# A two-layer conv and attention diffusion block: adaLN sums on four column parts of TensorE, and a rearranged start

## Chip, cores and metric

One core of one Trainium2 chip. The metric is device time in microseconds (us) of one execution; the kernel before takes 1625.7 us (median of 3 runs, 1624.08 to 1625.84).

## What is computed

The reference runs two layers over 512 latent tokens `x` and 256 context tokens `ctx`, width 1024. Layer 0 mixes tokens by a gated convolution of three taps, layer 1 by neighbourhood attention with 16 heads; each is followed by a SwiGLU with 2816 hidden columns. Every sub-layer is modulated by adaLN: a shift, a scale and a gate come from `silu(cond)` through one matrix per layer. Cut to that part:

```python
for i in range(DEPTH):
    mod   = jax.nn.silu(c)     @ w_ada[i] + b_ada[i]      # latent tokens:  1024 -> 6 * 1024
    mod_c = jax.nn.silu(c_ctx) @ w_ada[i] + b_ada[i]      # context tokens
    sh1, sc1, g1, sh2, sc2, g2 = jnp.split(mod, 6, axis=-1)   # and so for mod_c
    h = rms_norm(x, norm_mix[i]) * (1 + sc1) + sh1        # ctx the same way
    x = x + g1 * mixer(h)                                 # convolution (i = 0), attention (i = 1)
    x = x + g2 * swiglu(rms_norm(x, norm_ffn[i]) * (1 + sc2) + sh2)
```

## The kernel before

The streams lie transposed, features on partitions: `x` is eight tiles of 128 x 512, `c` eight of 128 x 256. Every large product is made of three matmuls: weights and activations are split into a high and a low part (`split`, L134 on ScalarE and L135 on VectorE; tiles `wh`/`wl` or `ah`/`al` for weights, `hxh`/`hxl` for the normed x), and `mm3` (L188) adds high*high, high*low and low*high in PSUM. A scheduler orders what is not pinned by `in_order`; loads go out on SP's queue, and their buffers (`raw`, three of 1 MB) set when.

**Start of layer 0.** SP loads x (8 x 256 KB), then the first adaLN weights (`first_load`, L224: `raw`, four rows of 256 columns to a partition and DMA, so rows of 1 KB), then the first conv weights (`first_weights`, L617: `fraw`, 12 x 256 KB, rows of 1 KB). The squares of x are taken on VectorE and ScalarE and added up on VectorE (L371 to L382), and `stats` (L394) sums them over partitions on TensorE, in four column parts j: output partitions 32j to 32j+31. `first_sum` (L236) computes 512 of the adaLN columns for both conditions with 32-column weights `cs` = silu(cond), in two parts (`part` 0 and 1) of 16 matmuls of 128 columns, for each column part j all k in a row:

```python
for j in range(4):
    for k in range(part * nk, part * nk + nk):
        matmul(ps[32*j:32*j+32, :wd], cs[:, k, :], raw[:, kk, ...])     # L236
```

`first_finish` copies the sum to SBUF (L243), transposes it (L246) and makes shift and gain (L254, L256). `spread` (L409) broadcasts the norm, `apply` (L425, L427, L428) makes `hxh` and `hxl`. A loop over q = 0 to 3 does this for two x tiles at a time: `apply`, then the conv products of those two tiles (j = 0, 1, 2 for the three column groups c, u, b), with the `first_sum` of the next two tiles set between them.

**The other adaLN columns** (`Ada.step`, `_step`): 40 steps of one 1 MB load each; VectorE multiplies and adds into `aa` for the latent condition (L286, L288), ScalarE and GpSimd do the same for the context (L291, L294, L295). Every four steps `flush` sums over partitions on TensorE (L309): up to four accumulators (two column blocks j, one or two conditions c), with the weights `ones2`, which put condition c in column c, so that both conditions add into the same 32 partitions:

```python
for c in range(1 + both):
    for j, (_, _, _, accs) in enumerate(two):
        matmul(ps[32*j:32*j+32, :], ones2[:, c, :], accs[c], start=(c == 0), stop=(c == both))   # L309
```

`finish` copies 64 partitions (L315), transposes them in four pieces (L318) and adds the bias (L324). Six flushes have two conditions, the last four have one.

**Where steps stand.** In `swiglu` a step follows each of the hidden tiles (`tt`), and for the chunks but the last `residual` calls `along` after output tiles f = 0, 2, 4 (flush and step) and 6 (flush). The hidden tiles come in chunks of 6, 8 and 8 in layer 0; after each chunk `residual` multiplies by the output weights.

Of the kernel before, what the change touches and what calls it, by code (L numbers as in the profile page):

```python
# [15 lines left out]
P = 128  # L16
# [21 lines left out]
def dit_kernel(  # L38
# [6 lines left out]
    w_ada: bass.AP,  # L45
    conv_w_in: bass.AP,
    conv_w_out: bass.AP,
# [37 lines left out]
    ones2 = const.tile([P, 2, 32], F32, name="ones2")  # L85
    nc.vector.memset(ones2, 0.0)
    nc.vector.memset(ones2[:, 0, 0:1], 1.0)
    nc.vector.memset(ones2[:, 1, 1:2], 1.0)
# [8 lines left out]


    x_t = [xr.tile([P, NX], F32, name=f"x{f}") for f in range(KT)]
# [17 lines left out]

    def in_order(inst):
        return tc.keep_in_program_order(inst)
# [89 lines left out]
    class Ada:  # L209
# [7 lines left out]
        def first_load(self, k0, n, part):  # L217

            nk = 8 // n
            raw = wp.tile([P, 2048], F32, name="raw", tag="raw")  # L220
            raw = raw.rearrange("p (k w c) -> p k w c", k=nk, w=2)
            for w in range(2):
                c0 = w * D + k0 * P
                in_order(nc.sync.dma_start(  # L224
                    out=raw[:, :, w, :], in_=w_ada[0, part * nk * P:(part + 1) * nk * P, c0:c0 + n * P].rearrange(
                        "(k p) c -> p k c", p=P)))
            return raw

        def first_sum(self, n, part, raw):
# [70 lines left out]
        def flush(self):  # L300
# [6 lines left out]
            for c in range(1 + both):  # L307
                for j, (_, _, _, accs) in enumerate(two):
                    in_order(nc.tensor.matmul(self.ps[32 * j:32 * j + 32, :], ones2[:, c, :], accs[c],  # L309
                                              start=(c == 0), stop=(c == both)))  # L310
            self.finish(i, q // 2)

        def finish(self, i, g):
            row = nrm.tile([P, 512], F32, name="row", tag="row", bufs=1)
            nc.scalar.copy(out=row[0:64, :], in_=self.ps[0:64, :])  # L315
# [4 lines left out]
            tv = tp[:, 0:256].rearrange("p (s j m) -> p j s m", s=4, j=2)  # L320
            ba = vt[:, V_BADA + i * 48 + g * 8:V_BADA + i * 48 + g * 8 + 8].rearrange("p (j s) -> p j s", j=2)
            conds = range(2 if i == 0 or g < 2 else 1)
            for cond in conds:
                nc.vector.tensor_tensor(  # L324
                    out=mod[i][:, cond, g * 8:g * 8 + 8].rearrange("p (j s) -> p j s", j=2),
                    in0=tv[:, :, :, cond], in1=ba, op=ALU.add)
# [31 lines left out]
    class Norm:  # L358
# [27 lines left out]
        def stats(self, use="mm", ordered=True, urgent=False):  # L386
# [3 lines left out]
            with tc.high_priority() if urgent else nullcontext():  # L390
                st = bank(use, "st")
                for p, part in enumerate([self.a] + self.parts):
                    for j in range(4):
                        m = nc.tensor.matmul(st[32 * j:32 * j + 32, 0:ch], ones, part[:, j * ch:(j + 1) * ch],  # L394
                                             start=(p == 0), stop=(p == self.apart))
                        if ordered:
                            tc.keep_in_program_order(m)
                nc.vector.tensor_scalar(out=v, in0=st[:, 0:ch], scalar1=1.0 / D, scalar2=EPS,
                                        op0=ALU.mult, op1=ALU.add)
                nc.scalar.activation(out=self.y, in_=st[:, 0:ch], func=AF.Ln, scale=1.0 / D, bias=eps)  # L400
                e = nc.scalar.activation(out=self.y, in_=self.y, func=AF.Exp, scale=-0.5)
                self.ready = (e.ins, newton(v, self.y).ins)
# [64 lines left out]
    def swiglu(tmp, ap_, i, groups, hs, chunks, ada=None, begin=None, norms=None, out=None, end=None, begin_norm=None):  # L467
# [25 lines left out]
        for ci, n_t in enumerate(chunks):  # L493
# [43 lines left out]
            while tt < n_t:  # L537
# [9 lines left out]
                if ada is not None:  # L547
                    ada.step()
# [4 lines left out]
            along = {0: ada.also, 2: ada.also, 4: ada.also, 6: ada.flush} if ada is not None and not last else None  # L553
# [4 lines left out]
    with ExitStack() as l0:  # L558
# [47 lines left out]
        def first_weights(q, j):  # L606
            part = (1, 2, 0)[j]
# [8 lines left out]
            raw = raw[:, :512].rearrange("p (k c) -> p k c", k=2)  # L616
            in_order(nc.sync.dma_start(  # L617
# [16 lines left out]
        for f in range(KT):  # L634
            nX.square(f, nc.vector)
# [461 lines left out]
```

## Time and profile before

| | us |
|---|---|
| median of 3 runs | 1625.7 |
| the profiled execution, its own time | 1626.88 |
| its span in the trace | 1625.1 |
| TensorE matmul busy | 1592.8 |
| VectorE busy | 858.7 |
| ScalarE busy | 578.5 |
| GpSimd busy | 243.7 |
| mean load rate over the span | 99 GB/s |

The span is what lies between the first and the last instruction; the profiled execution is 1.78 us longer than it and 1.18 us over the median. PE is TensorE's matmuls, PEld its weight loads, DVE VectorE, ACT ScalarE, POOL GpSimd, SP the engine that issues most loads. Times in views run from the start of the span. A product in float32 stands in the trace as two matmul records.

### The profile page before, as it was taken

To read this page: it belongs to the slowest core of one execution; us is meant where nothing else is said; L and a number is where in the kernel's file an instruction comes from. 1 tells how busy PE (TensorE), PEld (TensorE's weight loads), DVE (VectorE), ACT (ScalarE), POOL (GpSimd) and SP (SyncE) were. 2 spreads that over 40 slices of the span, in tenths; PEclk is the share of its full clock that TensorE was granted. 3 is DMA by queue.
4 is the path that set the end of the run, shared out by engine and by line. 5 is a ranking of instruction groups with operands and counts; after the bars stand their busy time and mean duration, and the time that the engine had idled before them with its cause. 6 is when DMAs were issued, how large, how long until landed. Compare 5 with 4: busy or idle time off the path is not lost.

```text
span 1625.1 us, 22151 instructions
## 1 busy us (share of the span) xinstructions
PE 1592.8 (98%) x9132; PEld 1341.0 (83%) x9132; DVE 858.7 (53%) x1395; ACT 578.5 (36%) x967; POOL 243.7 (15%) x290
## 2 busy tenths in 40 slices
PE   6999999999999999999999999999999999999998
PEld 5898888888888888888888778788878888888887
DVE  5467667476654435343522766666787533333333
ACT  4243234354423221122222555555655332222231
POOL 0123226323422000000003211121111000000000
PEclk9999999999999999999999999999999999999999
DMA  9423343234434334233411121110121232223222
GB/s 315 139 78 130 104 144 116 78 104 149 136 104 130 125 109 156 76 127 105 147 65 53 47 71 59 33 59 28 60 87 55 78 104 92 90 88 119 78 84 72
DMA packets 137077, 162.35 MB, mean 100 GB/s; under 512 B 3216, under 2 KB 114064, under 8 KB 136976
## 3 DMA queue, kind: packets, MB, share of 16 engines
q1 hardware_dynamic: 133504, 156.66, 29.5%
q10 hardware_dynamic: 3472, 4.28, 0.8%
q8 instruction: 71, 1.16, 0.3%
q14 instruction: 30, 0.25, 0.1%
HBM read 158.84 MB, written 2.10 MB: 99 GB/s over the span
## 4 chain that ended last, share of the span: by engine, by line
PE 93%; DVE 3%; ACT 1%; DMA 1%; issue 1%; POOL 0%; SPq 0%; DVEq 0%; ACTq 0%
PE ps L188 83%; PE op L919 2%; PE tp L909 1%; PE ada_ps L236 1%; PE s L889 1%; DMA raw<-in_w_ada_dram 1%; PE ada_ps L309 1%; PE s L890 1%; PE stt L803 1%; DVE wl L135 1%; DVE t L425 0%; PE bc L409 0%; DVE hxl L428 0%; DVE aa L288 0%; DMA x<-in_xT_dram 0%
## 5 line engine op out<-in xcount | busy, mean ns | idle before, releaser
L188 PE MATMUL ps<-hxh,wh 128*128 128x512 f32 (+1 forms) x1128 | 435.8, 392 | 3.1 <-DVE q_sb L857 1.3
L188 PE MATMUL ps<-hxl,wh 128*128 128x512 f32 (+1 forms) x1128 | 432.3, 389 | 1.3 <-DVE hxl L428 1.3
L188 PE MATMUL ps<-hxh,wl 128*128 128x512 f32 (+1 forms) x1128 | 431.5, 388 | 0.7 <-DVE wl L135 0.7
L134 ACT CAST wh<-raw 128x1024 fp32r<-128x1024 f32 (+1 forms) x194 | 198.1, 1022 | 465.6 <-PE ps L188 418.6
L135 DVE TENSOR_TENSOR wl<-raw,wh 128x1024 fp32r<-128x1024 f32 (+1 forms) x194 | 241.8, 1247 | 184.1 <-ACT wh L134 180.8
L188 PEld LDWEIGHTS ps<-hxh,wh 128*128 128x128 f32 x1128 | 211.0, 189 | 54.0 <-issue 3.6
L188 PEld LDWEIGHTS ps<-hxh,wl 128*128 128x128 f32 x1128 | 212.1, 188 | 44.9 <-DVE wl L135 1.8
L188 PEld LDWEIGHTS ps<-hxl,wh 128*128 128x128 f32 x1128 | 211.8, 188 | 43.2 <-DVE hxl L428 2.5
L188 PE MATMUL ps<-ah,wh 128*128 128x512 f32 (+1 forms) x656 | 232.3, 354 | 2.5 <-ACT ah L134 2.5
L188 PE MATMUL ps<-al,wh 128*128 128x512 f32 (+1 forms) x656 | 231.9, 354 | 0.4 <-DVE al L135 0.4
L188 PE MATMUL ps<-ah,wl 128*128 128x512 f32 (+1 forms) x656 | 231.1, 353 | 0.0
L188 PE MATMUL ps<-hch,wl 128*128 128x256 f32 x648 | 181.4, 284 | 0.0
L188 PE MATMUL ps<-hcl,wh 128*128 128x256 f32 x648 | 180.6, 283 | 0.0
L188 PE MATMUL ps<-hch,wh 128*128 128x256 f32 x648 | 179.3, 283 | 0.0
L288 DVE SCALAR_TENSOR_TENSOR aa<-raw,cs,aa 128x512 f32<-128x512 f32 x140 | 144.1, 1030 | 41.1 <-DMA raw<-in_w_ada_dram 38.0
L295 POOL TENSOR_TENSOR aa<-aa,pr 128x512 f32<-128x512 f32 x84 | 135.6, 1615 | 183.6 <-ACT pr L294 109.6
L188 PEld LDWEIGHTS ps<-ah,wh 128*128 128x128 f32 x656 | 123.8, 189 | 24.9 <-issue 3.8
L188 PEld LDWEIGHTS ps<-al,wh 128*128 128x128 f32 x656 | 123.7, 189 | 18.4 <-DVE al L135 0.6
L188 PEld LDWEIGHTS ps<-ah,wl 128*128 128x128 f32 x656 | 123.8, 189 | 17.5
L441 DVE SCALAR_TENSOR_TENSOR x<-ps,mod,x 128x512 f32<-128x512 f32 (+1 forms) x80 | 55.1, 695 | 143.6 <-PE ps L188 143.6
L188 PEld LDWEIGHTS ps<-hch,wh 128*128 128x128 f32 x648 | 122.4, 191 | 3.3 <-issue 0.8
L188 PEld LDWEIGHTS ps<-hcl,wh 128*128 128x128 f32 x648 | 123.1, 192 | 2.0 <-issue 0.2
(170 smaller groups left out, 1577.1 us busy)
## 6 DMA issues: line engine op xcount, KB each, us to landing
raw<-in_ffn_w_in_dram SPq DMA_DIRECT2D x44, 1024.0 KB, 5.1
raw<-in_w_ada_dram SPq DMA_DIRECT2D x40, 1024.0 KB, 5.2
raw<-in_ffn_w_out_dram SPq DMA_DIRECT2D x16, 1024.0 KB, 4.9
raw<-in_attn_w_qkv_dram SPq DMA_DIRECT2D x12, 1024.0 KB, 5.3
raw<-in_conv_w_in_dram SPq DMA_DIRECT2D x9, 1024.0 KB, 5.3
raw<-in_w_ada_dram SPq DMA_DIRECT2D x16, 512.0 KB, 7.8
raw<-in_ffn_w_out_dram SPq DMA_DIRECT2D x8, 768.0 KB, 4.3
raw<-in_conv_w_out_dram SPq DMA_DIRECT2D x4, 1024.0 KB, 4.9
```

The source lines that it names most:

```text
L134: a = pinned(nc.scalar.copy(out=hi, in_=src))
L135: b = pinned(nc.vector.tensor_tensor(out=lo, in0=src, in1=hi.bitcast(F32), op=ALU.subtract))
L188: m = nc.tensor.matmul(ps, w[k][part], src[k], start=(first and k == i == 0), stop=(last and k == nk - 1 and i == 2))
L236: in_order(nc.tensor.matmul(self.ps[32 * j:32 * j + 32, :wd], self.cs[:, k, :], raw[:, kk, j // 2, j % 2 * wd:(j % 2 + 1) * wd], start=(k ...
L288: nc.vector.scalar_tensor_tensor(out=acc, in0=raw[:, kk, :], scalar=w, in1=acc, op0=ALU.mult, op1=ALU.add)
L295: nc.gpsimd.tensor_tensor(out=acc, in0=acc, in1=pr, op=ALU.add)
L309: in_order(nc.tensor.matmul(self.ps[32 * j:32 * j + 32, :], ones2[:, c, :], accs[c], start=(c == 0), stop=(c == both)))
L441: nc.vector.scalar_tensor_tensor(out=grp.tiles[f], in0=ps, scalar=modv(i, grp.cond, gate, f), in1=grp.tiles[f], op0=ALU.mult, op1=ALU.add)
L803: nc.tensor.matmul(stt[row:row + 32, :], ind, sq, start=True, stop=True)
L889: nc.tensor.matmul(s, qh[a][:, bs], keys(ks[a], w0), start=True, stop=False)
L890: nc.tensor.matmul(s, ql[a][:, bs], keys(ks[a], w0), start=False, stop=True)
L919: in_order(nc.tensor.matmul(op_[own, 0:P], vv[:, vi, own], tps[a][:, j * P:(j + 1) * P], start=(j == 0), stop=(j == 3)))
```

## The change

1. `first_sum` runs over k outside and the column parts j inside, so that four neighbouring matmuls write four different column parts.
2. `flush` gives each of its up to four accumulators a column part of its own, with the weights `ones`; `ones2` goes. `finish` copies and transposes 128 partitions where it was 64 (64 stay 64 for the one-condition flushes).
3. The host lays out the first adaLN weights (`w_ada1`, 8 x 128 x 2048) and the first conv weights (`conv_w1`, 12 x 128 x 512) as they lie on chip. One DMA of 1 MB with rows of 8 KB takes the place of two of 512 KB; the conv DMAs have rows of 2 KB.
4. x is loaded over SP's and ACT's queues in turn, and the first two adaLN loads go out on ACT's queue.
5. `stats_of_each`: all eight squares of x on VectorE, each summed by four matmuls as it comes.
6. In the loop over q `apply` has high priority and the splits of the conv weights are ordered behind given instructions (`after`).
7. In `swiglu` the step after the last hidden tile of a chunk goes (not in the last chunk), and `along` has a step after f = 1, flush and step after 3 and 5, and the flush after 6.

```diff
@@ x and the first adaLN loads
+    def first_load(q, part, queue=None):
+        raw = wp.tile([P, 2048], F32, name="raw", tag="raw")
+        in_order((queue or nc.sync).dma_start(out=raw, in_=w_ada1[2 * q + part]))
+        return raw.rearrange("p (k w c) -> p k w c", k=4, w=2)
+
+    for f in range(KT):
+        in_order((nc.sync, nc.scalar)[f % 2].dma_start(out=x_t[f], in_=xT[f * P:(f + 1) * P, :]))
+    araw = [first_load(0, part, nc.scalar) for part in range(2)]
@@ first_sum
-            for j in range(4):
-                for k in range(part * nk, part * nk + nk):
-                    kk = k - part * nk
+            for k in range(part * nk, part * nk + nk):
+                kk = k - part * nk
+                for j in range(4):
@@ flush, finish
-            for c in range(1 + both):
-                for j, (_, _, _, accs) in enumerate(two):
-                    in_order(nc.tensor.matmul(self.ps[32 * j:32 * j + 32, :], ones2[:, c, :], accs[c],
-                                              start=(c == 0), stop=(c == both)))
+            for r, acc in enumerate(acc for _, _, _, accs in two for acc in accs):
+                in_order(nc.tensor.matmul(self.ps[32 * r:32 * r + 32, :], ones, acc, start=True, stop=True))
...
-                in_order(nc.tensor.transpose(out=tp[:, s * 64:(s + 1) * 64], in_=row[0:64, s * P:(s + 1) * P],
-                                             identity=ident[0:64, 0:64]))
+                in_order(nc.tensor.transpose(out=tp[:, s * nr:(s + 1) * nr], in_=row[0:nr, s * P:(s + 1) * P],
+                                             identity=ident[0:nr, 0:nr]))
@@ Norm
+        def stats_of_each(self, use):
...
+            for f, src in enumerate(self.grp.tiles):
+                sq = nrm.tile([P, NX], F32, name="sq", tag="sq")[:, :n]
+                nc.vector.tensor_tensor(out=sq, in0=src, in1=src, op=ALU.mult)
+                for j in range(4):
+                    in_order(nc.tensor.matmul(st[32 * j:32 * j + 32, 0:ch], ones, sq[:, j * ch:(j + 1) * ch],
+                                              start=(f == 0), stop=(f == KT - 1)))
@@ swiglu
-                if ada is not None:
+                if ada is not None and (tt < n_t - 1 or ci == len(chunks) - 1):
                     ada.step()
...
-            along = {0: ada.also, 2: ada.also, 4: ada.also, 6: ada.flush} if ada is not None and not last else None
+            along = {0: ada.also, 1: ada.step, 3: ada.also, 5: ada.also, 6: ada.flush} if ada is not None and not last else None
@@ first_weights, the loop over q
-            in_order(nc.sync.dma_start(
-                out=raw, in_=w_in[2 * q * P:2 * (q + 1) * P, part * D:part * D + 256].rearrange(
-                    "(k p) c -> p k c", p=P)))
+            in_order(nc.sync.dma_start(out=raw, in_=conv_w1[3 * q + j]))
...
-            split(wh, wl, raw)
+            split(wh, wl, raw, after)
...
-            nX.apply(hs[0], tiles=range(k0, k0 + 2))
+            nX.apply(hs[0], urgent=True, tiles=range(k0, k0 + 2))
```

How the rows move. **ACT's queue at the start**, before (x and all loads but one stand on SP):

```order
L79 DMA ct<-in_cst_dram 128x168
L563 ACT_TABLE_LOAD
L563 ACTIVATE cs<-vt 128x8
L564 ACTIVATE cs<-vt 128x8
L123 ACT_TABLE_LOAD
L380 ACTIVATE sq<-x_96 128x512
```

and with the change:

```order
L81 DMA ct<-in_cst_dram 128x168
L111 DMA x_91<-in_xT_dram 128x512
L111 DMA x_93<-in_xT_dram 128x512
L111 DMA x_95<-in_xT_dram 128x512
L111 DMA x_97<-in_xT_dram 128x512
L107 DMA raw<-in_w_ada_dram 128x2048 x2
L576 ACT_TABLE_LOAD
L576 ACTIVATE cs<-vt 128x8
L577 ACTIVATE cs<-vt 128x8
L131 ACT_TABLE_LOAD
L413 ACTIVATE y<-st,eps 128x128
L414 ACTIVATE y<-y 128x128
```

Six DMAs now stand ahead of silu(cond), and the squares have left ACT. SP's queue has four x loads, two conv loads and then the third adaLN load.

**VectorE at the end of layer 0's first SwiGLU chunk**, before (`aa_3969` is a step's accumulator, `al` a low part of the hidden tiles, `wl` of the output weights):

```order
L286 TENSOR_SCALAR aa_3969<-raw,cs 128x512
L288 SCALAR_TENSOR_TENSOR aa_3969<-raw,cs,aa_3969 128x512 x3
L486 TENSOR_TENSOR sg<-ps,sg 128x512
L288 SCALAR_TENSOR_TENSOR aa_3969<-raw,cs,aa_3969 128x512
L135 TENSOR_TENSOR al_3845<-sg,ah_3844 128x512
L288 SCALAR_TENSOR_TENSOR aa_3969<-raw,cs,aa_3969 128x512 x2
L135 TENSOR_TENSOR wl<-raw,wh 128x768
L288 SCALAR_TENSOR_TENSOR aa_3969<-raw,cs,aa_3969 128x512
L486 TENSOR_TENSOR sg<-ps,sg 128x256
L135 TENSOR_TENSOR wl<-raw,wh 128x768
L135 TENSOR_TENSOR al_3902<-sg,ah_3901 128x256
L441 SCALAR_TENSOR_TENSOR x_94<-ps,mod_91,x_94 128x512
```

and with the change:

```order
L282 TENSOR_SCALAR aa_4021<-raw,cs 128x512
L284 SCALAR_TENSOR_TENSOR aa_4021<-raw,cs,aa_4021 128x512 x3
L499 TENSOR_TENSOR sg<-ps,sg 128x512
L143 TENSOR_TENSOR al_3851<-sg,ah_3850 128x512
L143 TENSOR_TENSOR wl<-raw,wh 128x768
L499 TENSOR_TENSOR sg<-ps,sg 128x256
L143 TENSOR_TENSOR wl<-raw,wh 128x768
L143 TENSOR_TENSOR al_3908<-sg,ah_3907 128x256
L284 SCALAR_TENSOR_TENSOR aa_4021<-raw,cs,aa_4021 128x512
L454 SCALAR_TENSOR_TENSOR x_90<-ps,mod_87,x_90 128x512
L284 SCALAR_TENSOR_TENSOR aa_4021<-raw,cs,aa_4021 128x512 x2
L454 SCALAR_TENSOR_TENSOR c_98<-ps,mod_87,c_98 128x256
```

The second half of the step (the last four `aa`) stood among the splits and the last hidden tile; it now stands behind them.

**VectorE between q = 0 and q = 1**, before:

```order
L425 SCALAR_TENSOR_TENSOR t<-x_96,gain_93,bc 128x512
L425 SCALAR_TENSOR_TENSOR t<-x_97,gain_93,bc 128x512
L135 TENSOR_TENSOR wl<-fraw,wh 128x512 x2
L428 SCALAR_TENSOR_TENSOR hxl_127<-t,mod_91,hxh_119 128x512
L135 TENSOR_TENSOR wl<-fraw,wh 128x512
L428 SCALAR_TENSOR_TENSOR hxl_128<-t,mod_91,hxh_120 128x512
```

and with the change:

```order
L438 SCALAR_TENSOR_TENSOR t<-x_92,gain_89,bc 128x512
L438 SCALAR_TENSOR_TENSOR t<-x_93,gain_89,bc 128x512
L441 SCALAR_TENSOR_TENSOR hxl_135<-t,mod_87,hxh_127 128x512
L441 SCALAR_TENSOR_TENSOR hxl_136<-t,mod_87,hxh_128 128x512
L143 TENSOR_TENSOR wl<-fraw,wh 128x512 x6
```

All six weight splits now stand behind the two low parts of x.

## Rows read from the trace of the kernel before

**Rows 1.** The page: busy time by engine; the chain that ended last.

```profile
PE 1592.8 (98%) x9132; PEld 1341.0 (83%) x9132; DVE 858.7 (53%) x1395; ACT 578.5 (36%) x967; POOL 243.7 (15%) x290
...
PE 93%; DVE 3%; ACT 1%; DMA 1%; issue 1%; POOL 0%; SPq 0%; DVEq 0%; ACTq 0%
```

**Rows 2.** Windows: stretch, length, busy PE PEld DVE ACT POOL, PEclk, DMA, GB/s.

```profile
5.00:10.00 5.00, 0.00 (x0) 0.00 (x0) 3.35 (x5) 3.80 (x5) 0.00 (x0) 1.00 1.05 365
...
12.00:22.00 10.00, 7.98 (x89) 6.86 (x81) 3.53 (x12) 2.02 (x6) 0.00 (x0) 1.00 1.11 350
...
22.73:27.30 4.57, 4.57 (x13) 3.34 (x14) 3.80 (x6) 2.67 (x5) 0.00 (x0) 0.63 1.09 346
...
432.00:438.00 6.00, 3.13 (x14) 2.38 (x13) 5.74 (x8) 1.24 (x2) 1.78 (x1) 0.87 0.70 226
438.00:444.00 6.00, 6.00 (x31) 5.12 (x31) 0.92 (x2) 1.34 (x2) 0.00 (x0) 0.84 0.61 211
```

**Rows 3.** Chain of waits, 0 to 75 us: start, us, what.

```profile
12.84 5.96 PE ada_ps L236 x64
18.82 0.27 ACT row L243
...
20.47 0.60 DVE al L135
...
22.73 4.61 PE ps L188 x12
27.34 2.39 PE ada_ps L236 x32
```

**Rows 4.** DMA issues: the last load of the first adaLN weights; x's last.

```profile
raw<-in_w_ada_dram SPq DMA_DIRECT2D x1, 512.0 KB, 8.7
...
x<-in_xT_dram SPq DMA_DIRECT2D x2, 256.0 KB, 5.9
```

**Rows 5.** Timeline of TensorE and SP: start, us, engine line op.

```profile
7.77 0.80 SPq L224 DMA_DIRECT2D raw<-in_w_ada_dram  x1
...
11.75 0.66 PE L394 MATMUL st<-acc,ones 128*32 128x128 f32 x8 [11.75 <-DVE acc L382]
12.18 0.65 PE L394 MATMUL st<-sq,ones 128*32 128x128 f32 x8
...
39.16 0.19 PEld L188 LDWEIGHTS ps<-hxl,ah 128*128 128x128 f32 x1 [0.47 <-DVE hxl L428]
...
67.02 0.32 PE L394 MATMUL st<-acc,ones 128*32 128x64 f32 x8
67.15 0.29 PE L394 MATMUL st<-sq,ones 128*32 128x64 f32 x8
```

**Rows 6.** Timeline of TensorE: a flush with two conditions, one with one.

```profile
159.33 1.91 PE L309 MATMUL ada_ps<-aa,ones 128*32 128x512 f32 x8
...
609.55 1.05 PE L309 MATMUL ada_ps<-aa,ones 128*32 128x512 f32 x4
```

**Rows 7.** Timeline of TensorE: four transposes of 64 columns, four of 128.

```profile
403.75 0.46 PE L318 MATMUL ada_tp<-ct,row 64*128 64x64 f32 x4
...
955.58 0.60 PE L909 MATMUL tp<-ct,pt 128*128 128x128 f32 x4
```

**Rows 8.** Timeline of VectorE at the end of the first SwiGLU chunk.

```profile
425.94 0.75 DVE L288 SCALAR_TENSOR_TENSOR aa<-raw,cs,aa 128x512 f32<-128x512 f32 x1 [4.20 <-DMA raw<-in_w_ada_dram]
...
432.58 1.74 DVE L288 SCALAR_TENSOR_TENSOR aa<-raw,cs,aa 128x512 f32<-128x512 f32 x1
...
435.45 0.41 DVE L135 TENSOR_TENSOR al<-sg,ah 128x256 fp32r<-128x256 f32 x1
```

**Rows 9.** Timeline of TensorE in the same stretch.

```profile
435.16 0.38 PE L188 MATMUL ps<-ah,wh 128*128 128x256 f32 x1 [2.49 <-ACT ah L134]
435.92 0.39 PE L188 MATMUL ps<-al,wh 128*128 128x256 f32 x1 [0.38 <-DVE al L135]
436.50 0.63 PE L188 MATMUL ps<-al,wh 128*128 128x512 f32 x1
```

More of the change, by code (lines that the diff above doesn't have):

```diff
@@ L325, in finish @@
                     out=mod[i][:, cond, g * 8:g * 8 + 8].rearrange("p (j s) -> p j s", j=2),
-                    in0=tv[:, :, :, cond], in1=ba, op=ALU.add)
+                    in0=tv[:, :, :, cond, 0], in1=ba, op=ALU.add)
             if g not in (1, 4):
@@ L397, in stats, with root @@
                             tc.keep_in_program_order(m)
[L398 to L402, printed above, removed]
+                self.root(st, v)
+        def stats_of_each(self, use):
+            n, ch = self.grp.n, self.grp.n // 4
+            v = nrm.tile([P, P], F32, name="v", tag="v", bufs=1)[:, :ch]
+            self.y = nrm.tile([P, P], F32, name="y", tag="y", bufs=1)[:, :ch]
+            st = bank(use, "st")
+            for f, src in enumerate(self.grp.tiles):
[4 more added lines that the diff above has]
+                                              start=(f == 0), stop=(f == KT - 1)))
+            self.root(st, v)
+        def root(self, st, v):
+            ch = self.grp.n // 4
+            nc.vector.tensor_scalar(out=v, in0=st[:, 0:ch], scalar1=1.0 / D, scalar2=EPS,
+                                    op0=ALU.mult, op1=ALU.add)
+            nc.scalar.activation(out=self.y, in_=st[:, 0:ch], func=AF.Ln, scale=1.0 / D, bias=eps)
+            e = nc.scalar.activation(out=self.y, in_=self.y, func=AF.Exp, scale=-0.5)
+            self.ready = (e.ins, newton(v, self.y).ins)
         def spread(self, use="mm", ordered=True):
@@ L603, in conv, with first_weights @@
             srcs[g][1].append(al)
-        def first_weights(q, j):
-            part = (1, 2, 0)[j]
+        def first_weights(q, j, after=None):
             if q < 2:
@@ L631, in dit_kernel @@
         late, ws = {}, [[[], []] for _ in range(3)]
-        for f in range(KT):
-            in_order(nc.sync.dma_start(out=x_t[f], in_=xT[f * P:(f + 1) * P, :]))
-        for f in range(KT):
-            nX.square(f, nc.vector)
-        araw = [ada.first_load(0, 2, part) for part in range(2)]
-        nX.stats("aux")
+        nX.stats_of_each("aux")
         ada.first_sum(2, 0, araw[0])
@@ L645, in dit_kernel @@
             k0 = 2 * q
[L646 removed]
+            nX.apply(hs[0], urgent=True, tiles=range(k0, k0 + 2))
             if q == 0:
[L648 to L651 removed]
+                first_weights(0, 0, nX.ready)
+                first_weights(0, 1, nX.ready)
+                araw = [first_load(1, 0)]
+                first_weights(0, 2, nX.done[1])
                 for j in range(3):
[L653 to L654 removed]
+                    first_weights(1, j, nX.done[1])
+                araw.append(first_load(1, 1))
             elif q < 3:
@@ L659, in dit_kernel @@
                         for j in range(3):
-                            first_weights(2 + part, j)
-                    araw.append(ada.first_load(k0 + 2, 2, part))
+                            first_weights(2 + part, j, nX.done[3])
+                    araw.append(first_load(q + 1, part))
             else:
```

38 lines of the change are left out of this document (12 added, 26 removed).

## Prediction

> **What bounds the kernel now.** I read the page first: matmuls are busy for 98% of the span, and the chain that ended last runs through TensorE for 93% of it [rows 1]. So time is won only by TensorE work taken off, or by the few places where TensorE stands idle or runs at its lower clock. The windows show these: after the first products begin, the granted clock is 0.63 of full from 22.73 to 27.30, and around 435 us it is 0.87 and 0.84 (the lower of two levels, 1.2 of 2.4 GHz, for a part of the stretch), with matmuls busy for only 3.13 of 6.00 us [rows 2]. The chain through the first 75 us shows what the start consists of: adaLN sums, a copy, a split on VectorE, then products with further adaLN sums between them [rows 3]. Loads run at 350 GB/s with the DMA share at its top between 12 and 22 us [rows 2], so up to the first product the start is bound by loads as well.
>
> The sum below is made against the profiled execution's own time, 1626.9 us; the median of the runs, 1625.7, is 1.2 us lower. A measurement of this kernel tells some 0.2% (3 us) from no change.
>
> **Column sums between the first products.** Six parts of `first_sum` stand there, and the chain gives each 2.39 us for 32 records [rows 3]. That is some 21 steps of 0.11 us: with the four k of one column part in a row, only neighbours at the seams ran together. What four column parts do side by side is in the trace already: `stats` sends eight records of 128 columns in 12.18 - 11.75 = 0.43 us at the lower clock, 0.215 per four, and eight of 64 columns in 67.15 - 67.02 = 0.13 us at full clock [rows 5]. So a group of four with 128 columns takes 0.11 us at full clock. 32 records are eight groups, 0.9 us, and with the entry some 1.0. Six parts save 6 x (2.39 - 1.0) = **8.4 us**. They lie on the chain between products that are ready, so all of it counts. Bounds: nothing, if parts with different data don't run together (the `stats` matmuls share one weight tile, these do per k too), and 9.0 if the entry is free.
>
> Can the loads follow? The last first-stage adaLN load waits for a buffer that an earlier sum frees, so it moves forward with TensorE. Some 13.6 MB (x 2.1, adaLN 8.4, conv 3.1) at 350 GB/s [rows 2] take 39 us, and the last sums, before at 58.9, would stand near 50. Cover remains; if it went, each MB would cost 2.9 us.
>
> **Flushes.** Six flushes with two conditions take 1.91 us each, the one-condition flush 1.05 [rows 6]. The first has its four matmuls in two column parts, two deep; the second has two matmuls side by side. On four parts all four are one deep, so the price falls to the second: 6 x 0.86 = **5.2 us** saved. The four one-condition flushes keep their form. Against this the transposes widen from 64 to 128 columns: four take 0.60 instead of 0.46 us [rows 7], 6 x 0.14 = **0.8 us** lost. The copy of 128 partitions instead of 64 is on ScalarE, whose 578 us of 1625 [rows 1] leave room; it ends long before the transposes are due.
>
> **The stall at 432 us.** VectorE waited 4.20 us for the load of an adaLN step [rows 8]. Behind that step in its order stood the low parts of the last hidden tile and of the weights, and the last low part came at 435.45 [rows 8]. TensorE sat idle for 2.49 + 0.38 us [rows 9], and its clock fell: 6 x (0.13 + 0.16) = 1.74 us of clock were not granted in the 12 us that follow 432 [rows 2]. Together 4.6 us. In the changed order the step's second half stands behind those splits. What is late next: the residual add of the first output tile and one weight split wait behind it; the add's PSUM bank is one of seven, and the split is first needed three output tiles later. The steps' number stays the same (17 to the end of the first chunk instead of 18, then four with `along` instead of three), so a wait of the same kind could reappear at the new places; before, no other place in the SwiGLU of layer 0 had one. I take **4.6 us** saved, bounds 0 and 4.6.
>
> **VectorE between q = 0 and 1.** The wait of 0.47 us for `hxl` at 39.16 [rows 5] had three weight splits ahead of or between the two low parts; they now stand behind. **0.5 us** saved. The six splits in a row then stand before the next shift and gain, which are due only after two more sums and 24 products.
>
> **The start up to the first product** is where I am least sure. Before, the last DMA of the first adaLN weights was issued at 7.77 [rows 5] and landed 8.7 us later [rows 4], at 16.5; the sums ended at 18.8 and the first product ran at 22.73 [rows 3]. Now x goes over two queues, the adaLN loads stand on ACT's, and SP's goes on to conv weights at once.
>
> - Loads. What SP issues now moves beside the adaLN weights, where it stood behind them. If the queues take turns row by row, the first two conv loads (0.52 MB in rows of 2 KB against rows of 8 KB) come with them: 0.52 MB / 350 GB/s = +1.5 us. If they share bytes equally, 2.1 MB come with them: +6.0. If ACT's loads go first, 0. No row shows which; I take the first, the middle one, as no row is nearer. Longer rows are moved faster: x with 2 KB rows ran at 365 GB/s, the 1 KB rows at 350 [rows 2]; on 2.1 MB that is -0.3.
> - Sums. Before, 2.2 us lay between landing and the end of the sums; now 16 matmuls take 1.0 at full clock, twice that at the lower one: -0.2 to -1.2.
> - Broadcast: `bc` stands between the sums and the transpose on TensorE; at the lower clock its matmuls take about 1 us longer: 0 to +1. TensorE now has short bursts with gaps where it had one run, so the lower clock is likely; I take the middle of both.
> - The second split leaves the path of shift and gain: -0.6 [rows 3].
>
> Sum: 1.5 - 0.3 - 0.7 + 0.5 - 0.6 = **+0.4 us**, bounds -2.4 and +6.1. At nothing I cost: the squares (x's last tile landed 5.9 us after its issue at 4.5 [rows 4]; two squares, a sum and the root follow, some 4 us, and end by 14.5, three before the adaLN sums do); the six DMA issues on ACT ahead of silu(cond) (ready by about 11.5, first used at 15); the fourteen DMA issues fewer on SP, which never were the bound.
>
> The Trainium skill, "DMA: Bandwidth & Descriptors", section "Issuing engines are not separate DMA queues", says that DMAs started from different engines run on the same 16 engines and interleave, so that two queues save issue time alone. The 350 GB/s at full share [rows 2] agree. By that page x over two queues would give nothing here, and what SP moves beside the adaLN weights would be paid for by them, which is the second rival.
>
> **Sum.** 8.4 + 5.2 - 0.8 + 4.6 + 0.5 - 0.4 = 17.5 us. 1626.9 - 17.5 = 1609.4 on the profiled execution, less 1.2: **1608.2 us** as the median.
>
> **Rivals.**
> 1. The forecast, chance 0.58: about 1608.2, its own range 1604.5 to 1611 (bounds of the start as far as no wait takes its place).
> 2. The queues share bytes: the first adaLN weights land some 6 us later, the first product at about 27, 4.5 us worse than forecast: 1612.7. For: SP's loads are issued as soon as a few x tiles have landed. Against: rows of 8 KB may win over rows of 2 KB. Chance 0.2.
> 3. The stall moves instead of going: the step's second half now holds up the residual adds and a weight split until its load lands. Its full price is 4.6 us: 1612.8. For: the same three buffers serve steps and weights. Against: three output tiles of time. Chance 0.11.
> 4. The column parts don't run together for the adaLN sums, so the change doesn't do what it says: 8.4 us stay, and the flushes' 5.2 in part: 1608.2 + 8.4 + 2.6 = 1619. Against it stand `stats` and the one-condition flush [rows 5, 6]. Chance 0.07.
> 5. Slower than before: TensorE, with short bursts and waits on loads at the start, is kept at its lower clock through the whole first stage. A product of 512 columns then takes 0.43 instead of 0.23 us. The point from which it decides: 17.5 / 0.2 = 88 products at the lower clock; with all 144 of the stage it would cost 29 us: 1637. Against: before, the clock came back within the first twelve products, with products back to back [rows 2]. Chance 0.04.
>
> **Numbers.** The predicted time is that of the likeliest case, 1608.2. The range holds the forecast and rivals 2 and 3 with the start's bounds, 1604 to 1614.5. Faster by over 0.2% means below 1622.5, where cases 1 to 4 lie, less a little for 4 with a late start: 0.95; within 0.2%: 0.02; slower: 0.03.
>
> **What would show it.** In the changed profile: the 32 records of each later `first_sum` in about 1.0 us; the two-condition flush at about 1.05; no idle time of TensorE and full clock at the end of the first SwiGLU chunk; no wait for `hxl` after q = 0; the first product within a us of 22.7. The prediction is wrong if the first product comes at 26 or later, if the sums keep 2.39 us, or if a new wait for an adaLN load shows on VectorE in layer 0's residuals.

## The result and the profile after

The changed kernel takes **1607.3 us** (median of 4 runs, 1604.9 to 1608.0) against 1625.3 of the kernel before beside it: ratio 0.9887, 95% interval 0.9875 to 0.9899, so 18.0 us less. The forecast was 1608.2. The profiled execution took 1604.90 us (span 1603.0), the lowest of the four and 2.4 below their median; that of before (1626.88) lay 1.6 over its median. The two profiles therefore differ by 22.0 us, the medians by 18.0, and where the other 4 us are is part of what follows.

The page of the changed kernel, busy time by engine and the chain, beside [rows 1]:

```profile
PE 1576.2 (98%) x9180; PEld 1327.1 (83%) x9180; DVE 858.2 (54%) x1392; ACT 573.3 (36%) x961; POOL 242.9 (15%) x290
...
PE 94%; DVE 2%; ACT 1%; DMA 1%; issue 1%; POOL 0%; ACTq 0%; POOLq 0%; SPq 0%; DVEq 0%
```

TensorE lost 16.6 us of busy time and bounds as before. Windows of the changed kernel (stretch, length, busy PE PEld DVE ACT POOL, PEclk, DMA, GB/s): the loads, the first twelve products, and the end of the first SwiGLU chunk, beside [rows 2]:

```profile
12.00:22.00 10.00, 6.32 (x94) 4.66 (x95) 5.91 (x15) 4.01 (x9) 0.00 (x0) 1.00 1.03 411
20.90:25.20 4.30, 4.30 (x14) 2.93 (x14) 3.80 (x6) 2.68 (x5) 0.00 (x0) 0.66 1.02 399
...
417.00:423.00 6.00, 6.00 (x36) 5.23 (x35) 2.27 (x5) 1.45 (x3) 0.44 (x1) 1.00 0.52 175
```

The end of the chunk, 3.13 busy of 6.00 and a clock of 0.87 before, is now 6.00 of 6.00 at 1.00. The loads run at 411 GB/s where they ran at 350. The chain of waits of the changed kernel (start, us, what), beside [rows 3]:

```profile
7.49 9.11 DMA raw<-in_w_ada_dram
...
16.64 1.08 PE ada_ps L232 x32
17.72 1.09 PE bc L422 x8
...
20.90 4.36 PE ps L196 x12
25.26 1.23 PE ada_ps L232 x32
...
28.08 1.01 PE ada_ps L232 x32
...
37.84 4.86 DMA c<-in_ctxT_dram
...
43.14 0.76 ACT sq L375 x2
43.90 0.62 ACT hxh L440
```

A later part of `first_sum` takes 1.01 us, where it took 2.39 (the first of the six, still partly at the lower clock, 1.23). There is a wait that the kernel before did not have: the squares of `c` on ScalarE stand ahead of the high part of x that the products of the third pair of x tiles need. TensorE on the timeline, a flush with two conditions and its transposes, and a flush with one, beside [rows 6, 7]:

```profile
149.57 1.07 PE L304 MATMUL ada_ps<-aa,ones 128*32 128x512 f32 x8
156.16 0.60 PE L313 MATMUL ada_tp<-ct,row 128*128 128x128 f32 x4
...
589.01 1.05 PE L304 MATMUL ada_ps<-aa,ones 128*32 128x512 f32 x4
```

And the timeline of VectorE at the end of the first chunk, beside [rows 8]:

```profile
417.49 0.41 DVE L143 TENSOR_TENSOR al<-sg,ah 128x256 fp32r<-128x256 f32 x1
421.64 0.75 DVE L284 SCALAR_TENSOR_TENSOR aa<-raw,cs,aa 128x512 f32<-128x512 f32 x1 [3.73 <-DMA raw<-in_w_ada_dram]
422.31 0.74 DVE L454 SCALAR_TENSOR_TENSOR x<-ps,mod,x 128x512 f32<-128x512 f32 x1
```

VectorE still waits 3.73 us for the step's load, but the last low part (417.49) now comes ahead of that wait. What stands behind it is a residual add, and TensorE does not wait for that: it is busy for all of 417 to 423 us.

The lead of the changed profile at milestones that both kernels have. The first two columns are times in us from the span's start; the last is what the lead grew by since the row above:

| milestone on TensorE | before | after | gained since the last |
|---|---|---|---|
| first product | 22.73 | 20.90 | 1.83 |
| second adaLN sum of the next pair | 31.25 | 28.01 | 1.41 |
| first flush | 159.33 | 149.57 | 6.52 |
| fourth flush | 396.09 | 383.53 | 2.80 |
| sixth flush | 540.20 | 520.69 | 6.95 |
| seventh flush | 609.55 | 589.01 | 1.03 |
| end of the last matmul | 1620.96 | 1599.26 | 1.16 |

### The profile page after: what moved, and what is told of

It is laid out like the page before. It is cut to its first block, busy times and chain, and to the rows that moved or that the text cites. A ratio compares the mean times of both kernels' runs of the same rounds, so it can differ in the third digit from the quotient of the medians.

```text
span 1603.0 us, 22223 instructions
## 1 busy us (share of the span) xinstructions
PE 1576.2 (98%) x9180; PEld 1327.1 (83%) x9180; DVE 858.2 (54%) x1392; ACT 573.3 (36%) x961; POOL 242.9 (15%) x290
## 3 DMA queue, kind: packets, MB, share of 16 engines
q8 instruction: 72, 1.18, 0.3%
## 4 chain that ended last, share of the span: by engine, by line
PE 94%; DVE 2%; ACT 1%; DMA 1%; issue 1%; POOL 0%; ACTq 0%; POOLq 0%; SPq 0%; DVEq 0%
PE ps L196 86%; PE op L925 2%; PE tp L915 1%; PE s L895 1%; PE s L896 1%; PE stt L809 1%; PE ada_ps L304 1%; DMA raw<-in_w_ada_dram 1%; PE bc L422 0%; PE ada_ps L232 0%; DVE t L438 0%; DMA x<-in_xT_dram 0%; DVE wl L143 0%; ACT hxh L440 0%; DMA c<-in_ctxT_dram 0%
```

## Experiments

All are the changed kernel with one edit, unless it says otherwise, timed in four or five runs. Ratios are to the kernel before, timed beside it on the same chip, with 95% intervals. Differences in us to the changed kernel are to its median of 1607.3; once more (run 9) it had 1606.3, and its eight times lie between 1604.9 and 1608.2. So a difference of up to 2 us rests on the traces and not on the medians.

**1. The old order of the sums.**

```diff
-            for k in range(part * nk, part * nk + nk):
-                kk = k - part * nk
-                for j in range(4):
+            for j in range(4):
+                for k in range(part * nk, part * nk + nk):
+                    kk = k - part * nk
```

> The changed kernel with the old order in the adaLN sums of the first stage (column parts outside, k inside); every engine's order is otherwise the same. Theory (the win there comes only from neighbours that write different column parts, and lies wholly on the path): the six later sums go back from 1.08 to about 2.4 us each, +8 us, and the second of the first two sums, which waits for its load, ends 1.2 us later: +9.2 us in all, median about 1616.5, first product near 22.1. Rival (the loads bind behind the sums, so that slower sums cost less): below +5 us, median below 1612.3, and waits for the adaLN load on TensorE get shorter by what the sums grow.

Measured: 1614.1 us, 0.9932 (0.9920 to 0.9945), 6.8 more than the changed kernel, between the theory and its rival. Its timeline of TensorE:

```profile
13.36 5.71 PE L232 MATMUL ada_ps<-raw,cs 128*32 128x128 f32 x64
19.00 1.16 PE L422 MATMUL bc<-y,pick 128*128 128x128 f32 x8
...
26.80 2.46 PE L232 MATMUL ada_ps<-raw,cs 128*32 128x128 f32 x32
```

Each part costs 2.46 again where it was 1.08, six times 1.38, so 8.3. That the median moved by 6.8 has two reasons in the rows. TensorE is at full clock from the sums on (`bc` in 1.16), after slow sums that kept it busy up to there without a pause, so the first product comes at 22.26 and not later. And the wait behind c's squares is gone: c lands in time for a path that is later. The gain of the new order is on the path. The adaLN loads don't bind behind it, but 0.6 us of it turn into that wait.

**2. The old flush** (two column parts, two deep; 64 rows copied and transposed).

```diff
-            for r, acc in enumerate(acc for _, _, _, accs in two for acc in accs):
-                in_order(nc.tensor.matmul(self.ps[32 * r:32 * r + 32, :], ones, acc, start=True, stop=True))
+            for c in range(1 + both):
+                for j, (_, _, _, accs) in enumerate(two):
+                    in_order(nc.tensor.matmul(self.ps[32 * j:32 * j + 32, :], ones2[:, c, :], accs[c], ...))
...
```

> The changed kernel with the old flush (two column parts, two accumulators deep, 64 rows copied and transposed). Theory from the two traces: each of the six two-condition flushes costs 0.98 us more, its transposes taken in: +5.9 us, median about 1613.2. Rival (the prediction's terms: 0.86 more for the matmuls, 0.14 less for the transposes): +4.4 us, median about 1611.7. If the flushes are hidden: 1607.3. The durations of the six flushes and of their transposes in the trace decide between the first two, which the medians hardly can.

Measured: 1613.5 us, 0.9931 (0.9919 to 0.9944), 6.2 more. From its first flush to its last matmul the trace is 6.0 us longer than that of the changed kernel. From a flush's start to the product behind it there are 1.841 us against 0.996: 0.845 each. From the first transpose to the product behind the four there are 0.388 us with 64 rows and 0.354 with 128. The wider transposes cost nothing on the path.

**3. The old places of the steps.**

```diff
-                if ada is not None and (tt < n_t - 1 or ci == len(chunks) - 1):
+                if ada is not None:
                     ada.step()
...
-            along = {0: ada.also, 1: ada.step, 3: ada.also, 5: ada.also, 6: ada.flush} if ...
+            along = {0: ada.also, 2: ada.also, 4: ada.also, 6: ada.flush} if ...
```

> The changed kernel with the steps of adaLN columns where they stood before in the SwiGLU of layer 0. Theory (the wait of VectorE for the step's load holds back the low parts behind it): the stall returns at the end of the first chunk, near 415 us of the span, with 2.9 us of idle TensorE and a stretch at the lower clock of 3.4 us (1.7 us lost): +4.8 us, median about 1612.1. Rival A (the idle time returns but the lower clock does not): +3.0 us. Rival B (the earlier start and the shorter flushes let the load come in time): no stall, 1607.3.

Measured: 1613.7 us, 0.9928 (0.9915 to 0.9940), 6.3 more. The stall is back and larger. Its timeline of VectorE, that of TensorE, and two windows:

```profile
416.72 0.75 DVE L284 SCALAR_TENSOR_TENSOR aa<-raw,cs,aa 128x512 f32<-128x512 f32 x1 [4.81 <-DMA raw<-in_w_ada_dram]
```

```profile
425.91 0.46 PE L196 MATMUL ps<-ah,wh 128*128 128x256 f32 x1 [4.68 <-ACT ah L142]
426.67 0.58 PE L196 MATMUL ps<-al,wh 128*128 128x256 f32 x1 [0.31 <-DVE al L143]
```

```profile
420.00:426.00 6.00, 1.31 (x12) 1.11 (x10) 6.00 (x5) 1.85 (x3) 4.38 (x3) 1.00 0.19 60
426.00:432.00 6.00, 5.69 (x20) 4.46 (x21) 2.72 (x5) 0.83 (x1) 0.00 (x0) 0.72 0.97 318
```

Idle 4.68 + 0.31 and 6 x 0.28 of clock: 6.7 us, against 4.6 in [rows 2, 9]. TensorE arrives here 11.4 us earlier than before (421.23 against 432.67), the step's load only 9.2 (416.72 against 425.94). So the move is worth more with the other parts than alone.

**4. x and the first adaLN loads on one queue, ahead of the conv loads.**

```diff
-        in_order((nc.sync, nc.scalar)[f % 2].dma_start(out=x_t[f], ...))
-    araw = [first_load(0, part, nc.scalar) for part in range(2)]
+        in_order(nc.sync.dma_start(out=x_t[f], ...))
+    araw = [first_load(0, part) for part in range(2)]
```

> The changed kernel with x and the first two adaLN loads all on SP's queue, in front of the first conv loads. Theory (the 16 DMA engines are shared, so what counts is which bytes stand ahead of the adaLN weights; issue time is covered): the conv loads no longer run beside the adaLN loads, these land up to 2 us earlier (second one at 14.6 to 16), first product 19 to 20.5, median 1605.5 to 1607. Rival (two queues are what made the start shorter): x and the adaLN loads come later by the issue time of six more DMAs on one queue, some 2 to 4 us: first product 22 to 24, median 1609 to 1611.

Measured: **1604.9 us** (1604.2 to 1605.0), 0.9874 (0.9859 to 0.9889), 2.5 less than the changed kernel and 1.4 less than its repeat; the intervals of the ratios overlap. Its chain of waits:

```profile
5.69 9.54 DMA raw<-in_w_ada_dram
...
15.27 1.93 PE ada_ps L232 x32
17.20 1.91 PE bc L422 x8
...
21.20 4.60 PE ps L196 x12
```

The second adaLN load lands at 15.22, 1.4 to 1.8 us earlier than with two queues, though x is issued later. The Trainium skill, "DMA: Bandwidth & Descriptors", section "Issuing engines are not separate DMA queues", says that queues of several engines save issue time alone. The trace agrees: the issue of these ten loads was covered, and the second queue only let other bytes run beside those that were waited for. The first product came at 21.20, 0.7 later than expected, because sum and broadcast ran at the lower clock.

**5. The old rows of 1 KB, on the new queues** (`first_load` by two DMAs from `w_ada`, `first_weights` from `w_in`, as before; queues and order unchanged).

> The changed kernel with the first adaLN and conv weights loaded as before, from the weights as given (rows of 1 KB, two DMAs of 512 KB for one of 1 MB), over the same queues in the same order. Theory (the rate of the loads depends on the length of their rows: 350 GB/s with 1 KB against 400 to 434 with 8 and 2 KB): the second adaLN load lands 1.5 to 2.5 us later than in the runs with long rows, near 18.5 to 19.5 us, and the first product follows it: median 1609 to 1610. Rival A (row length matters little, as the prediction had it with 0.3 us): 1607.3 to 1608. Rival B (the queues share row by row, so short rows on both sides let the conv loads take more): 1611 or above, the second adaLN load at 21 or later.

Measured: 1612.0 us, 0.9920 (0.9905 to 0.9935), 4.7 more: the time and the landing of rival B. A window, then the chain:

```profile
12.00:22.00 10.00, 4.46 (x52) 2.17 (x52) 2.92 (x7) 3.96 (x8) 0.00 (x0) 1.00 1.10 349
```

```profile
10.97 11.44 DMA raw<-in_w_ada_dram
...
28.58 4.33 PE ps L200 x12
```

Two things show. The rate is 349 GB/s, where the host layout gives 411 (its rows are longer and lie side by side; no run parts the two). And the last part of the adaLN weights lands at 22.4, six us after the 16.5 of before with the same rows on one queue. That is the price that the prediction gave to queues that share bytes: with equal rows on both queues, they do (0.68 MB on ACT's queue and 0.71 on SP's from 14 to 18 us). Rows of 8 KB against rows of 2 KB take the larger share: in run 7 a conv load of 256 KB issued at 5.03 landed at 11.68, an adaLN load of 1 MB issued at 5.23 on the other queue at 12.88. From 9.4 to 11.6 us of that run the two queues (q10 is ACT's, q1 SP's) moved this (packets, MB, share of 16 engines):

```profile
q10 hardware_dynamic: 96, 0.75, 81.8%
q1 hardware_dynamic: 88, 0.17, 19.9%
```

A packet in these rows is one row of a load, so the queues had nearly as many rows each, and the bytes went as four to one. The Trainium skill, "DMA: Bandwidth & Descriptors", section "Queues, rings and completion order", says that each engine goes round between its queues packet by packet. The equal counts agree; how many rows an engine takes before it goes on is not shown. Rival B was right in its mechanism too.

**6. One adaLN load on each queue**, x over both.

```diff
-    araw = [first_load(0, part, nc.scalar) for part in range(2)]
+    araw = [first_load(0, part, (nc.sync, nc.scalar)[part]) for part in range(2)]
```

> The changed kernel with x over two queues as it is, but the first two adaLN loads one on each queue, so that on SP one stands ahead of the first conv loads. Theory (what counts is the bytes that run beside or ahead of the adaLN loads, not the number of queues): the second adaLN load lands at 14.3 to 15.4 as with all on one queue, median 1604.3 to 1605.3. Rival (one queue is faster by itself): the second load lands at 16 or later, median 1606.5 to 1607.5.

Measured: 1606.9 us, 0.9884 (0.9868 to 0.9901). My theory missed; its rival's numbers came. The chain:

```profile
4.66 11.05 DMA raw<-in_w_ada_dram
15.84 3.64 PE ada_ps L232 x64
...
23.66 4.43 PE ps L196 x12
```

The two loads share, so the first lands at 15.71 (12.70 on one queue) and the second at 15.99, and both sums run behind them. One queue brings the loads in the order in which they are needed, so that in run 4 the first sum was done before the second load was there. By the medians run 4 is 2.0 us faster; how much of that is the order and how much the bytes kept away, no run parts. Why the second load itself is 0.8 later than on one queue stays open.

**7. c's squares behind the third pair's high parts.**

```diff
-                nc.scalar.activation(out=sq, in_=src, func=AF.Square)
+                m = nc.scalar.activation(out=sq, in_=src, func=AF.Square)
+                if after is not None:
+                    behind(m.ins, after)
...
-                    nC.square(f, nc.gpsimd)
+                    nC.square(f, nc.gpsimd, nX.done[5][0])
```

> The changed kernel with the squares of c on ScalarE ordered behind the high parts of the third pair of x tiles. Theory (the wait of 0.6 us for these high parts comes from c's squares standing ahead of them in ScalarE's order): TensorE runs through between the second and the third pair, -0.6 us, median about 1606.7. Rival (the high parts wait for VectorE's t anyway, or c's statistics come late in return): no change, 1607.3, or up to 0.5 us more. The trace decides; the start of this kernel is that of the changed one, so its first product also shows how far that differs from run to run (20.9 to 23.2 expected).

Measured: 1605.6 us, 0.9880 (0.9865 to 0.9894); the medians can't tell it from no change, the trace can. The chain runs through 24 products without a wait:

```profile
43.55 5.50 PE ps L196 x24
```

From the transpose to the next sum it is 5.70 us, in the changed kernel 6.38 (6.27 in run 9): some 0.6 less, and c's statistics aren't late for it.

**8. Filler on TensorE up to the first product** (71 small matmuls of constants into a bank that nothing reads: 24 ahead of the first statistics, 3 before each of the other seven, 12 between the first two sums, 14 ahead of the first product).

> The changed kernel with filler on TensorE up to the first product: 71 small matmuls of constants into a bank that nothing reads. Theory (TensorE's short bursts leave it at the lower clock, and with the filler it is at the full one by the time of the adaLN sums): second adaLN sum and broadcast in 1.08 and 1.16 us instead of 1.94 and 2.08, the first twelve products in 2.9 instead of 4.6: -2.5 to -3.5 us, median 1604 to 1605. Rival A (the clock falls with the first products whatever was before): only the sum and the broadcast gain, -1.5 us, median near 1605.8. Rival B (the filler delays the statistics, or the waits on loads stay long enough for the clock to fall): 1607 or above.

Measured: 1606.2 us, 0.9884 (0.9869 to 0.9899). Its chain:

```profile
16.16 2.51 PE spare L118 x23
...
19.65 1.09 PE bc L431 x8
20.85 3.17 PE spare L118 x28
24.02 3.00 PE ps L204 x12
```

Both theory and rival B: sums and `bc` are at full clock, the first twelve products take 3.00 us where they took 4.4 to 4.6, and the filler, which I had made too long, gives most of it back. It holds up the second sum by 0.6 us, and the first product starts at 23.95, 1.2 us after its operand (`hxh`, begun at 22.06, takes 0.73).

**9. The changed kernel once more.**

> The changed kernel itself, once more, for its profile and beside the next ones. Theory (its first profile was an early start: the runs of four kernels with the same start had their first product at 20.9, 22.7, 23.2 and 23.2 us): first product at 22.5 to 23.3, second adaLN sum and broadcast at the lower clock, 1606.5 to 1608. Rival (that profile is the rule): first product at 20.9, 1605.

Measured: 1606.3 us (four runs: 1605.1, 1605.3, 1607.3, 1608.2), 0.9883 (0.9868 to 0.9898); the profiled one was 1605.28. TensorE:

```profile
13.29 1.93 PE L232 MATMUL ada_ps<-raw,cs 128*32 128x128 f32 x32
16.97 1.08 PE L232 MATMUL ada_ps<-raw,cs 128*32 128x128 f32 x32 [1.74 <-DMA raw<-in_w_ada_dram]
17.98 1.16 PE L422 MATMUL bc<-y,pick 128*128 128x128 f32 x8
```

An early start again (first product at 21.23), so against my theory for this run. But runs 2 and 3 have the same code up to the first product (run 2 but for three small constants set on VectorE) and show the other form. Run 3, first product at 23.24:

```profile
12.92 1.94 PE L232 MATMUL ada_ps<-raw,cs 128*32 128x128 f32 x32 [1.18 <-ACT y L414]
17.10 1.94 PE L232 MATMUL ada_ps<-raw,cs 128*32 128x128 f32 x32 [2.24 <-DMA raw<-in_w_ada_dram]
18.96 2.08 PE L422 MATMUL bc<-y,pick 128*128 128x128 f32 x8
```

Sum and broadcast run at either clock, and the first product comes at 20.9 to 21.2 or at 22.7 to 23.2 us (run 7 in between in its broadcast, 22.74). The eight times of the changed kernel are three from 1604.9 to 1605.3 and five from 1606.8 to 1608.2, which fits; no profile of one of the five exists, so that they are the late form is inferred.

The rows show a difference further ahead. In the two early profiles x's last tile landed at 11.1 and 11.4 us, and the statistics on TensorE run into the first sum without a pause. In runs 2, 3, 7 and 10 it landed at 9.4 to 9.6 us, TensorE then stood idle for 1.18 to 1.32 us ahead of the first sum, and second sum and broadcast began at the lower clock. So x came earlier and the first product later. No run changed this alone, so that it is the cause is not shown.

**10. Without priority and splits' order.**

```diff
-            nX.apply(hs[0], urgent=True, tiles=range(k0, k0 + 2))
+            nX.apply(hs[0], tiles=range(k0, k0 + 2))
...
-            split(wh, wl, raw, after)
+            split(wh, wl, raw)
```

> The changed kernel without the priority of the shift and gain and without the splits' order. Theory (the weight splits get ahead of the path again): the four splits of the first pair stand among shift and gain, +0.6 to +1.5 us at the first product, and the high parts of the second pair stand behind six splits on ScalarE, which end about 36.5 where these high parts were due at 32: up to +2 us there. Median 1608.5 to 1610.5. Rival (the weights' loads set when the splits run, and the orders change nothing on the path): 1607.3. Rival B (only the wait for the low part goes or comes, as in the prediction): +0.5 us, 1607.8.

Measured: 1608.6 us (1607.8 to 1608.8), 0.9895 (0.9881 to 0.9910), 1.3 to 2.3 more than the two medians of the changed kernel. The chain:

```profile
8.41 11.39 DMA fraw<-in_conv_w_dram
...
19.83 0.63 ACT ah L142
...
20.48 0.52 DVE al L143
...
24.12 5.20 PE ps L196 x12
```

A conv weight's load and split stand in the way of shift and gain; from the second sum's start to the first product it takes 7.35 us, in run 3, at the same clock, 6.14. The order is worth 1.2 us there. The twelve products behind take 5.20 us, in run 3 4.62, because here the lower clock lasts to the last of them; whether the order has to do with that is open. The wait for the low part after the first pair, which the prediction put down to the splits among the low parts, did not come back: from the transpose to the next sum it is 5.80 us here, 5.78 in the changed kernel, 6.08 before. In this run the six splits stand ahead of the pair's shift and gain, so what is shown is only that the order of the changed kernel is not needed against that wait.

**11. Runs 4 and 7 together, and the broadcast between the first two sums.**

```diff
         ada.first_sum(2, 0, araw[0])
+        nX.spread("aux")
         ada.first_sum(2, 1, araw[1])
-        nX.spread("aux")
```

> The changed kernel with x and the first adaLN loads on one queue, c's squares behind the third pair's high parts, and the broadcast between the first two adaLN sums. Theory (the parts add): -2.4 and -0.7 us as measured for the first two, and the broadcast in the gap in front of the second sum, -0.5 us at the lower clock: median about 1603.8. Rival (the broadcast now delays the second sum at the lower clock by as much): 1604.3 or above.

Measured: 1604.1 us, 0.9869 (0.9854 to 0.9883), within 0.3 of the theory and of its rival alike, so the median does not decide. In the trace the rival's delay is there: at the lower clock the broadcast (2.08 us) ends after the second load has landed (15.01), and that sum starts at 16.52. What it costs there it saves behind, with the first product at 20.48, 0.7 earlier than in run 4.

**12. The same with filler that fits.**

> The kernel of the run before with filler on TensorE, sized so that it ends before what it would hold up: nine small matmuls ahead of the first statistics, one before each of the others, five ahead of the first adaLN sum, seven between transpose and first product. Theory (full clock from the adaLN sums on, nothing delayed): second sum ends at 16.3, first product at 18.8 to 19.5, first twelve products in 2.9 us: median 1600 to 1601.5. Rival A (so little filler does not bring the clock up): as the run without it, 1603.8. Rival B (the filler holds up the statistics or the sums): 1602 to 1604 at full clock, with the first product at 20 or later.

Measured: **1602.6 us** (1602.1 to 1603.4), 0.9861 (0.9844 to 0.9877), 1.5 below run 11, and with its slowest run below every run of the changed kernel. TensorE:

```profile
12.64 1.08 PE L240 MATMUL ada_ps<-raw,cs 128*32 128x128 f32 x32 [0.26 <-DMA raw<-in_w_ada_dram]
...
15.07 1.08 PE L240 MATMUL ada_ps<-raw,cs 128*32 128x128 f32 x32 [0.26 <-DMA raw<-in_w_ada_dram]
...
19.93 0.73 PE L204 MATMUL ps<-hxh,ah 128*128 128x512 f32 x2 [0.93 <-ACT hxh L453]
```

Full clock throughout, nothing held up by the filler. The first product is 0.4 later than I expected: its chain now goes through a conv load (landing 16.16) and two splits, which stand among shift and gain again. That explains 0.4 of the 1.1 us by which the median lies above the range that I gave. Another 0.4 is a new wait, for the high part of the last pair:

```profile
53.23 0.74 PE L204 MATMUL ps<-hxh,wh 128*128 128x512 f32 x2 [0.43 <-ACT hxh L453]
```

Among this pair's shift and gain on VectorE now stand multiplications of an adaLN step, whose load came in just before; runs 8 and 11 have the same wait (0.23 and 0.38 us). The rest is not settled.

## Why the prediction was right

1608.2 was forecast and 1607.3 measured, inside the likeliest case's own range. By its terms:

- **Column sums, 8.4.** 1.01 us a part where 1.0 was taken, but for the first in the changed profile (1.23). The trace of before held the price in [rows 5]; run 1 shows that neighbours in different column parts are what does it. Part of the gain was given back: 0.64 us to the wait behind c's squares, which the prediction had not seen (run 7). It asked whether loads could follow, for the adaLN weights alone; c's load and its squares were on the path next.
- **Flushes, 5.2 less 0.8.** The matmuls gave 6 x 0.845 = 5.1. The term for the transposes was wrong, in sign too: 0.60 against 0.46 us in [rows 7] are busy times whose end is modelled. What counts is when the next product starts, and that is 0.354 against 0.388. Run 2 puts the part at 6.0, where the two terms made 4.4; of the 6.0 these rows hold 5.3, and the rest is spread.
- **The stall, 4.6.** In the pair of profiles 4.95: the 6.95 of the table hold two flushes as well, which gave 1.03 and 0.97. The rival that the stall moves fell: the residual add waits in its place and TensorE does not. Undone, the move costs 6.3 by the medians and 6.7 by the rows (run 3). One sign of being wrong was "a new wait for an adaLN load" on VectorE in layer 0's residuals. Taken by its words it came up, 3.73 us at 421.64; it is the old wait in a new place and costs TensorE nothing, so the sign was worded too widely.
- **The wait for the low part, 0.5.** 0.3 of it went, and not, as put, because of the splits' order (run 10).
- **The start, +0.4.** Two forms: 1.5 to 1.8 us earlier than before in the profiles of the changed kernel, 0.0 to 0.5 later in runs 2, 3 and 7. The middle that was taken between the two clocks is between the two forms. The landing was 0.1 to 0.6 later (+1.2 was taken): the queues did take turns row by row (run 7), and the host layout gave 411 GB/s for 350, not the 365 of x's rows. The path from the transpose to the product shrank from 3.02 to 2.26, by 0.76, where 0.6 was taken. "Within a us of 22.7" holds for the late form alone. The bounds given for this term, -2.4 and +6.1, don't follow from its parts, which make -2.1 and +5.9. What the squares of x on VectorE (point 5 of the change) are worth by themselves no run shows.
- **Rival 2, shared bytes,** is what happens with rows of 1 KB (run 5). The host layout kept it away: without it the new queues would have lost six us at the first sums. The prediction gave the layout 0.3 us.
- Rivals 4 and 5: the column parts do run together, and the lower clock ended with the twelfth product or in the sum behind it.

So the main mechanisms held, and that the sum is only 0.9 us off is in part luck: the flushes gave 1.6 more than their terms, the sums lost 0.6 of theirs again, and the start swings by some 2 us between its two forms.

The profiles differ by 22.0 and the medians by 18.0. The early form of the start makes some 2 us of that, and 1.2 more are a stretch of 3.41 us at the lower clock, from 1259.10 to 1262.51, that only the profile of before has.

## What to carry to other kernels

Small matmuls with few output columns of the array in use should be issued so that neighbours write different column parts; the price of four together can be read from any place where it is done already. Loads that the first work waits for were best on one queue in the order of need, with long rows that lie side by side, and nothing beside them; a second queue gained nothing here, where the issue time was covered. When a path gets shorter, look at what stands ahead of it in the in-order queues of the engines that feed it, since an operand that came in time before, like c's squares, can be the next wait.

## What the runs showed of the hardware that was not expected

The rate of loads followed their layout: 349 GB/s with rows of 1 KB, 409 to 411 with rows of 8 and 2 KB that lie side by side, all at a DMA share above 1.0. Two queues with equal rows shared the engines evenly (run 5, 0.68 and 0.71 MB in 4 us); with 8 KB against 2 KB the queues moved nearly as many rows each, and so four bytes to one (run 7). The granted clock in the windows reads 1.00 at 12 to 22 us in runs whose matmuls, by their spacing, ran at half speed (run 4: 1.93 us for a sum that takes 1.08). The first clock record of that trace begins at 18.88 us, and a stretch without a record reads 1.00: there the duration of a known matmul is the better clock. In run 8 the filler went from 0.43 to 0.22 us a matmul at about 6.3 us, after it had run from 1.04 us without a pause, and stayed there. What decides between the two forms of the start is not settled: TensorE was idle for 1.69 and 1.74 us ahead of the second sum in the early ones and for 2.24 in run 3, but in run 4 a wait of 0.5 us went with the lower clock. Ahead of the first sum it was not idle in the early ones, and for 1.1 to 1.3 us in runs 2, 3, 4, 7 and 10.
